# A fused two-layer block on one core: a position bias table made later, a triangle of ones loaded and copied earlier

## The chip, the core and the metric

The kernel runs on one core of a Trainium2 chip. Its engines have a queue each, which they work through in order: TensorE (PE, matmuls and transposes; its weight loads are PEld), VectorE (DVE), ScalarE (ACT), GpSimd (POOL) and SyncE (SP, which here only issues DMAs). The metric is the device time of one execution in microseconds (us), the median of several runs.

## The reference, cut to what matters

Two transformer blocks run one after the other on 512 tokens of width 1024, in float32. The change lies in the first 60 us of the first block, its input projection and the start of its attention:

```
xn   = rmsnorm(x, attn_norm_g)                       # 512 x 1024
proj = xn @ w_in                                     # 1024 -> 2312 columns
qa, ka, va, qb, kb, vb, f_logit = split(proj)
# mixer A: 8 heads, 2 key heads, window 128, a position bias per head, sinks
scores = qa . ka / 8  - 2^-(h+1) * dist              # dist = query - key, 0..127
out_a  = softmax with sink(scores) @ va
# mixer B: 8 heads, causal, forget gates
log_f  = log_sigmoid(f_logit + b_forget)             # 512 x 8
c      = cumsum(log_f, over tokens)
out_b  = softmax(qb . kb / 8 + c[t] - c[s], causal) @ vb
x      = x + concat(out_a, out_b) @ w_out
x      = x + relu(rmsnorm(x) @ w_up)^2 @ w_down
```

The second block (modulated norms, a pooling mixer, neighbourhood attention over the 512 tokens and a context, a second MLP) follows and isn't touched.

## The kernel before

Every float32 matmul is done as three passes: each operand is split into a rounded high part and a low rest, and `mm3` (lines 155 to 158) multiplies high by high, high by low and low by high into one accumulator. `split` (149 to 152) makes the parts: ACT copies to the high part, DVE (or POOL) subtracts for the low one.

`attention_one` does norm, projection and both mixers. The tokens stand in four tiles of 128 (t = 0 to 3). The projection is done in six chunks c of 384 or 392 columns (two for mixer A, four for B). `project(c, finish)` holds the loop: the weights of a chunk come in four pieces kp (`load`, `part_of`, 256 rows each), a raw DMA into one of two buffers, then a multiply by the norm's gain (L187 and L188, or on POOL, L185, for two of the four pieces) into a ring of five pairs `w_kp h/l`. For chunk 0 tiles 0 and 1 are multiplied as their tokens arrive, then tiles 2 and 3 one after the other. Each accumulator lies in one of two PSUM banks, so the matmuls of tile 2 need the bank that the eviction of tile 0 frees. The eviction is `close(t)`: one ACT operation (L411) that writes `pjs` and scales by the token's norm `r1[t]`, made by ACT (L260, a sum of squares) and two POOL operations (L208, L209). Then `finish` computes head norms on POOL, transposes q and k on PE (`ta`, L494) and evicts them as parts on ACT and DVE (L468 to L478). Between tile 2 and tile 3 the weights of the next chunk are loaded.

After chunk 0 the program makes the bias table `tab` (named alibi, L746: eight ACT copies of a 128x256 distance matrix `alibi0`, each with its head's slope), which DVE's pass over the scores `sa` (L609) adds. Then `gates()` turns the eight forget columns `zf` into log-sigmoids (Exp and Ln on ACT, L545 and L546), spreads them to `lfx`, splits that to `lfh`, and sums over tokens by a matmul `cps` (L562) with a triangle of ones `trir`: 896 columns loaded raw (`traw`, L556) and cast by DVE (L558). `lfx`, `traw` and `chl` come from one ring of three buffers (`prob("l", ..)`), `lfh` and `trir` from another (`prob("h", ..)`), in the order in which the program draws them; the input tiles `xin` and two raw weight pieces used the same rings before.

From there on attention of mixer A runs interleaved with the projection of the next chunk (generators, `interleave`), then mixer B with the rest.

The order in each engine's queue isn't that of the program. A planner runs the whole program at build time on a simulated clock and gives each engine, at each moment, the oldest of the operations that it holds for ready. Waits between engines are added afterwards. `tc.issue_after(ins)` is a rule for the planner: operations traced in its block on the engine of `ins` are queued behind `ins`; it adds no wait.

Of the kernel before, what the change touches and what calls it, by code (L numbers as in the profile page):

```python
# [8 lines left out]
F32 = mybir.dt.float32  # L9
F32R = mybir.dt.float32r  # L10
AF = mybir.ActivationFunctionType
# [5 lines left out]
P = 128  # L17
# [16 lines left out]
C_TRI = 384  # L34
# [99 lines left out]
class Build:  # L134
# [172 lines left out]
    def attention_one(self, ph):  # L307
        tc, nc, a = self.tc, self.nc, self.a
        tp = ph.enter_context(tc.tile_pool(name="t1", bufs=2, reuse_waits="tile"))
        cst = a["consts"]  # L310
        ac = nc.scalar.activation
# [3 lines left out]
        def const(name, shape, dt=F32):  # L315
            return tp.tile(shape, dt, name=name, tag=name, bufs=1)

        def prob(which, name, shape, dt=F32R):
            return tp.tile(shape, dt, tag="pt" + which, name=name, bufs=3)
# [17 lines left out]
        def load(c):  # L337
            tiles = []
            for kp in range(4):
                rv, (n, w, gain) = part_of(c, kp)  # L340
                tiles.append(self.parts(f"w{c}_{kp}", rv, n, w, gain, nc.gpsimd if c > C1 and kp in KPG else None))
                yield 0.0
            loaded[c] = tiles
# [18 lines left out]
        r1 = const("r1", [P, NT])  # L362
# [16 lines left out]
        alibi0 = const("alibi0", [P, 256])  # L379
# [9 lines left out]
        def project(c, finish):  # L389

            n = sum(w for _, w in segs[c])
            if c and c not in loaded:
                yield from load(c)
            tiles = loaded.pop(c) if c else []
            accs = {}

            def part(t, kp):
                if kp == 0:
                    accs[t] = self.ps("x", f"pj{c}_{t}")
                cols = slice(t * P, (t + 1) * P)  # L400
                wh, wl = tiles[kp]
                for i in range(2):
                    k = 2 * kp + i
                    xq = xnT[k // 4]
                    self.mm3(accs[t][:, 0:n], xq[:, k % 4, 0, cols], xq[:, k % 4, 1, cols], wh[:, i, :], wl[:, i, :],
                             k == 0, k == KC - 1)
                    yield 0.48

            def close(t):
                s = tp.tile([P, 392], F32, tag="pj", name=f"pjs{c}_{t}", bufs=2)  # L410
                ac(out=s[:, 0:n], in_=accs[t][:, 0:n], func=AF.Copy, scale=r1[:, t:t + 1])  # L411
                finish(t, s)

            def square(t):
                self.inv_rms(xin[t], r1, t, f"r1_{t}", self.part("wl", f"xs{t}", F32))

            turns = range(NT)
            if c == 0:
                turns = (2, 3)
                for kp in range(4):  # L420
                    if kp < 2:
                        self.split_T(xin[kp], xnT, kp, f"n1_{kp}")
                    rv, (a_, w, gain) = first[kp]
                    tiles.append(self.parts(f"w0_{kp}", rv, a_, w, gain))
                    if kp == 0:
                        yield from part(0, 0)
                    else:
                        if kp == 1:
                            yield from part(0, 1)
                            yield from part(1, 0)  # L430
                            yield from part(1, 1)
                        else:
                            square(kp - 2)
                            yield from part(0, kp)
                            yield from part(1, kp)
                for t in (2, 3):
                    self.split_T(xin[t], xnT, t, f"n1_{t}")
                for t in range(2):
                    close(t)
                    square(t + 2)  # L440
            for t in turns:
                for kp in range(4):
                    yield from part(t, kp)
                close(t)
                if t == NT - 2 and c + 1 < len(segs):
                    yield from load(c + 1)

        def head_norm(s, nh, name):

            w = 64 * nh  # L450
            sq = tp.tile([P, 384], F32, tag="sq", name=name + "sq", bufs=1)
            nc.gpsimd.tensor_tensor(out=sq[:, 0:w], in0=s[:, 0:w], in1=s[:, 0:w], op=ALU.mult)
            ss = self.small("ss", name + "ss")
            nc.vector.tensor_reduce(out=ss[:, 0:nh], in_=sq[:, 0:w].rearrange("p (h d) -> p h d", h=nh), axis=AX.X, op=ALU.add)
            r = self.rstd(ss[:, 0:nh], nh, 64, name + "r")
            qn = tp.tile([P, 384], F32, tag="qn", name=name + "qn", bufs=2)
            nc.gpsimd.tensor_tensor(out=qn[:, 0:w].rearrange("p (h d) -> p h d", d=64),
                                    in0=s[:, 0:w].rearrange("p (h d) -> p h d", d=64),
                                    in1=r[:, 0:nh].unsqueeze(2).to_broadcast([P, nh, 64]), op=ALU.mult)
            return qn  # L460
# [43 lines left out]
        def project_a(i):  # L504
            pa = Pairs(f"ta{i}")

            def finish(t, s):
                if i == 0:
                    nc.vector.tensor_tensor(out=zf[:, t, :], in0=s[:, 384:392], in1=bfor, op=ALU.add)
                qn = head_norm(s, 5, f"a{i}{t}")  # L510
                self.split(va[i][0][:, t, 0:64], va[i][1][:, t, 0:64], s[:, 320:384])
                pa.put(t, [qn[:, 0:P], qn[:, P:2 * P], qn[:, 2 * P:2 * P + 64]])
                if t % 2 == 1:
                    cols = slice((t - 1) * P, (t + 1) * P)
                    for h in range(4):
                        put_q(qa[4 * i + h], pa.get(h // 2), gn["q_norm_a"], h % 2, cols)
                    put_k(*ka[i], pa.get(2), gn["k_norm_a"], 0, cols, True)
            yield from project(i, finish)
# [22 lines left out]
        def gates():  # L541

            az = const("az", [P, NT, 8])
            stt(out=az, in0=zf, scalar=-1.0, in1=zf, op0=ALU.mult, op1=ALU.max)
            ac(out=az, in_=az, func=AF.Exp, scale=-1.0)  # L545
            ac(out=az, in_=az, func=AF.Ln, bias=1.0)  # L546
            stt(out=zf, in0=zf, scalar=0.0, in1=az, op0=ALU.min, op1=ALU.subtract)
            lfx = prob("l", "lfx", [P, NT, P], F32)
            lfh = prob("h", "lfh", [P, 2, NT, P])
            nc.gpsimd.memset(lfx, 0.0)  # L550
            for t in range(NT):
                nc.vector.tensor_copy(out=lfx[:, t, 0:32].rearrange("p (h r) -> p h r", r=4),
                                      in_=zf[:, t, :].unsqueeze(2).to_broadcast([P, 8, 4]))
            self.split(lfh[:, 0], lfh[:, 1], lfx)
            traw = prob("l", "traw", [P, 896], F32)
            nc.sync.dma_start(out=traw, in_=cst[:, C_TRI:C_TRI + 896])  # L556
            trir = prob("h", "trir", [P, 896])
            nc.vector.tensor_copy(out=trir, in_=traw)  # L558
            cps = self.ps("s", "cps")
            for t in range(NT):  # L560
                for part in range(2):
                    mm(out=cps, lhsT=lfh[:, part, t, :], rhs=trir[:, 384 - 128 * t:896 - 128 * t],  # L562
                       start=(t == 0 and part == 0), stop=(t == NT - 1 and part == 1))
            chl = prob("l", "chl", [P, 2, SEQ])
            self.split(chl[:, 0], chl[:, 1], cps)
            for dst, o in ((bq, 0), (bk, 3)):
                tmp = tp.tile([P, SEQ], F32, tag="p", name=f"btmp{o}", bufs=3)
                nc.vector.tensor_scalar(out=tmp, in0=chl[:, 0].bitcast(F32), scalar1=coef[:, o:o + 1],
                                        scalar2=coef[:, o + 2:o + 3], op0=ALU.mult, op1=ALU.add)
                stt(out=dst, in0=chl[:, 1].bitcast(F32), scalar=coef[:, o + 1:o + 2], in1=tmp, op0=ALU.mult, op1=ALU.add)  # L570
# [168 lines left out]
                    values(u, h)  # L739
                    yield CB * 0.8  # L740

        for _ in project_a(0):
            pass
        tab = self.gp.tile([P, 8, 256], F32, tag="g", name="alibi")
        for h in range(8):
            ac(out=tab[:, h, :], in_=alibi0, func=AF.Copy, scale=-(2.0 ** -(h + 1)))  # L746
        mixT.append(self.quad("mixT0"))
        b = {}
        gates()
        interleave(attn_a((0, 1)), project_a(1), RA[0])  # L750
        interleave(attn_a((2, 3)), project_b(0, b), RA[1])
# [799 lines left out]
```

## Time and profile before

| | |
|---|---|
| three runs | 1253.91, 1253.65, 1258.92 us, median 1253.91 |
| profiled execution | 1258.2 us, its span 1256.4 us, mean granted clock of PE 0.987 |
| PE busy | 1211.0 us, 96% of the span |
| DVE, ACT, POOL busy | 843.2 us (67%), 594.2 us (47%), 256.4 us (20%) |
| PE in the 40 slices of the span | 7899999998999999999999999999899999999997 |
| DMA | 155.42 MB, mean 124 GB/s |

A slice is 31.4 us and a digit its busy share in tenths. Busy shares are averages over stages with different limits: PE is the fullest engine in nearly all of them. In a timeline a row is one operation or several like it: start, length, engine, line, operation, tile written and tiles read, shapes, count, and in brackets the idle time of the engine ahead of it with what ended that.

### The profile page before, as it was taken

What the parts mean: (1) busy time and instruction counts of PE and PEld (TensorE: products, weight loads), DVE (VectorE), ACT (ScalarE), POOL (GpSimd) and SP (SyncE); (2) the same over time, 40 slices, a digit from 0 to 9 for tenths busy, and PEclk for the clock granted to TensorE, in tenths of its full rate; (3) what the DMA queues carried; (4) which work ended last, traced back from release to release, by engine and by line L of the source; (5) the groups of instructions that cost most, each with busy time, mean ns of one, the idle gap of its engine ahead of it and who ended that gap; (6) DMA issues with size and microseconds to landing.
All of it is one profiled execution on the core that took longest, in us unless ns stands there. A gap on an engine that the chain in (4) does not pass through costs nothing. (4 is left out here: it accounts for less than half of the span.)

```text
span 1256.4 us, 16975 instructions
## 1 busy us (share of the span) xinstructions
PE 1211.0 (96%) x6304; PEld 1013.8 (81%) x6304; DVE 843.2 (67%) x1461; ACT 594.2 (47%) x1103; POOL 256.4 (20%) x324
## 2 busy tenths in 40 slices
PE   7899999998999999999999999999899999999997
PEld 6898888788888878888889878777798888888775
DVE  3798776497988864346355557574867568578675
ACT  5576655434323313225245546463566454453442
POOL 2787552243010000000013224030600000000000
PEclk8998999999999999999999999999999999999998
DMA  6221222355668744234145311315355535436331
GB/s 165 64 59 46 66 63 68 101 167 149 206 217 258 235 138 141 67 101 135 67 151 158 85 51 53 102 38 201 119 189 161 166 86 177 142 98 187 101 101 67
DMA packets 154154, 155.42 MB, mean 124 GB/s; under 512 B 14489, under 2 KB 115624, under 8 KB 154072
## 3 DMA queue, kind: packets, MB, share of 16 engines
q1 hardware_dynamic: 149096, 143.08, 37.4%
q0 software_dynamic: 4400, 10.22, 2.6%
q8 instruction: 49, 0.80, 0.3%
q10 hardware_dynamic: 576, 1.05, 0.2%
q14 instruction: 33, 0.27, 0.1%
HBM read 147.96 MB, written 6.36 MB: 123 GB/s over the span
## 5 line engine op out<-in xcount | busy, mean ns | idle before, releaser
L902 DVE SCALAR_TENSOR_TENSOR macc<-mod,silu_c,macc 128x1024 f32<-128x1024 f32 x56 | 76.7, 1379 | 14.1 <-DMA mod<-in_w_mod_dram 14.1
L1453 POOL TENSOR_TENSOR ss<-ss,nhalf 128x1 f32<-128x1 f32 x4 | 3.0, 740 | 332.8 <-DVE ss L1452 332.8
L1305 DVE TENSOR_TENSOR m2d<-m2d,m2d 128x1024 f32<-128x1024 f32 x28 | 34.1, 1222 | 21.9 <-DMA m2d<-in_w_mlp_out_dram 21.8
L979 DVE SCALAR_TENSOR_TENSOR xa<-m1d,r,xa 128x512 f32<-128x512 f32 x32 | 23.8, 746 | 35.3 <-PE m1d L158 35.3
L151 ACT ACTIVATE m1hid<-m1sq 128x512 fp32r<-128x512 f32 x32 | 20.0, 630 | 37.4 <-DVE m1sq L848 37.4
L922 POOL DMA_DIRECT2D modrows<-mrow x8 | 3.9, 492 | 144.4 <-DVE mrow L920 90.2
L152 DVE TENSOR_TENSOR npl<-t,nph 128x512 fp32r<-128x512 f32 x32 | 21.7, 680 | 16.4 <-ACT nph L151 16.3
L152 DVE TENSOR_TENSOR m1hid<-m1sq,m1hid 128x512 fp32r<-128x512 f32 x32 | 21.9, 686 | 9.1 <-ACT m1hid L151 9.1
L185 POOL TENSOR_SCALAR w<-w,g_attn 128x384 f32<-128x384 f32 x20 | 25.6, 1290 | 8.9 <-DMA w<-in_w_in_dram 6.3
L687 DVE TENSOR_REDUCE mb<-sb 128x1 f32<-128x128 f32 (+3 forms) x32 | 15.6, 486 | 16.7 <-PE sb L684 16.6
L198 POOL TENSOR_SCALAR p<-p,d 128x512 f32<-128x512 f32 x8 | 14.0, 1752 | 55.8 <-DVE d L1120 26.5
L1119 ACT ACTIVATE p<-s,m 128x512 f32<-128x512 f32 x32 | 22.0, 689 | 5.8 <-DVE m L1117 5.8
L689 ACT ACTIVATE pb<-sb,mb 128x128 f32<-128x128 f32 (+3 forms) x32 | 16.8, 526 | 15.8 <-DVE mb L687 15.5
L847 ACT ACTIVATE m1re<-m1up 128x512 f32<-128x512 f32 x32 | 18.7, 583 | 11.0 <-PE m1up L158 11.0
L156 PE MATMUL pj<-w_0h,xnT 128*128 128x384 f32 (+1 forms) x48 | 18.5, 386 | 4.5 <-ACT pjs L411 3.3
L151 ACT ACTIVATE nph<-t 128x512 fp32r<-128x512 f32 x32 | 19.1, 596 | 7.4 <-PE t L1130 7.2
L1073 POOL TENSOR_TENSOR tb<-G,nam 128x256 f32<-128x256 f32 x24 | 17.8, 774 | 22.3 <-DVE m L1113 12.5
L848 DVE SCALAR_TENSOR_TENSOR m1sq<-m1up,m1re 128x512 f32<-128x512 f32 x32 | 21.8, 682 | 0.0
L1270 ACT ACTIVATE m2sq<-m2up 128x512 f32<-128x512 f32 x32 | 18.7, 584 | 6.5 <-PE m2up L158 6.5
L1331 DVE TENSOR_TENSOR y<-m2p,y 128x512 f32<-128x512 f32 x32 | 21.1, 682 | 0.2 <-PE m2p L158 0.2
L1272 ACT ACTIVATE m2sq<-m2sq 128x512 f32<-128x512 f32 x32 | 20.2, 633 | 0.9
L151 ACT ACTIVATE pbh<-tb 128x128 fp32r<-128x128 f32 (+3 forms) x32 | 13.7, 435 | 14.5 <-PE tb L707 14.4
(2045 smaller groups left out, 4624.3 us busy)
## 6 DMA issues: line engine op xcount, KB each, us to landing
m2d<-in_w_mlp_out_dram SPq DMA_DIRECT2D x53, 512.0 KB, 3.7
mod<-in_w_mod_dram SPq DMA_DIRECT2D x48, 512.0 KB, 4.4
m1u<-in_w_up_dram SPq DMA_DIRECT2D x32, 512.0 KB, 4.4
m1d<-in_w_down_dram SPq DMA_DIRECT2D x32, 512.0 KB, 3.6
m2u<-in_w_mlp_in_dram SPq DMA_DIRECT2D x32, 512.0 KB, 4.1
w<-in_w_in_dram SPq DMA_DIRECT2D x16, 512.0 KB, 4.0
w<-in_w_in_dram SPq DMA_DIRECT2D x48, 128.0 KB, 2.6
o1w<-in_w_out_dram SPq DMA_DIRECT2D x8, 512.0 KB, 3.7
```

Of the source, the lines that this page charges most:

```text
L151: self.nc.scalar.activation(out=hi, in_=src, func=AF.Copy)
L152: (eng or self.nc.vector).tensor_tensor(out=lo, in0=src, in1=hi.bitcast(F32), op=ALU.subtract)
L185: eng.tensor_scalar(out=rv[:, i], in0=rv[:, i], scalar1=g, scalar2=None, op0=ALU.mult)
L847: ac(out=r, in_=acc, func=AF.Relu)
L848: nc.vector.scalar_tensor_tensor(out=s, in0=acc, scalar=0.0, in1=r, op0=ALU.max, op1=ALU.mult)
L902: nc.vector.scalar_tensor_tensor(out=accs[s], in0=rw, scalar=sc[:, s, k:k + 1], in1=accs[s], op0=ALU.mult, op1=ALU.add)
L979: nc.vector.scalar_tensor_tensor(out=x[t][:, cols], in0=acc, scalar=r2[:, t:t + 1], in1=x[t][:, cols], op0=ALU.mult, op1=ALU.add)
L1119: ac(out=pr, in_=s, func=AF.Exp, bias=m[:, 2:3], accum_out=den[:, 0:1])
L1270: ac(out=s, in_=acc, func=AF.Relu)
L1272: ac(out=s, in_=s, func=AF.Square)
L1305: tt(out=o, in0=x, in1=z, op=ALU.subtract)
L1331: tt(out=Y[n][tau], in0=acc, in1=Y[n][tau], op=ALU.add)
```

## The change

It does three things. `close` keeps its eviction instruction in `self.closed`. The table's eight copies are traced in a block that queues them behind the last such eviction of chunk 0, that of tile 3. The draw, load and cast of the triangle move from the middle of `gates()` into the first projection: behind 32 steps of its generator, that is after the first half of tile 3's matmuls, behind the loads of chunk 1's weights.

```diff
             def close(t):
                 s = tp.tile([P, 392], F32, tag="pj", name=f"pjs{c}_{t}", bufs=2)
-                ac(out=s[:, 0:n], in_=accs[t][:, 0:n], func=AF.Copy, scale=r1[:, t:t + 1])
+                self.closed = ac(out=s[:, 0:n], in_=accs[t][:, 0:n], func=AF.Copy, scale=r1[:, t:t + 1])
                 finish(t, s)
...
             self.split(lfh[:, 0], lfh[:, 1], lfx)
-            traw = prob("l", "traw", [P, 896], F32)
-            nc.sync.dma_start(out=traw, in_=cst[:, C_TRI:C_TRI + 896])
-            trir = prob("h", "trir", [P, 896])
-            nc.vector.tensor_copy(out=trir, in_=traw)
             cps = self.ps("s", "cps")
...
-        for _ in project_a(0):
+        first_a = project_a(0)
+        for _ in range(32):
+            next(first_a)
+
+        traw = prob("l", "traw", [P, 896], F32)
+        nc.sync.dma_start(out=traw, in_=cst[:, C_TRI:C_TRI + 896])
+        trir = prob("h", "trir", [P, 896])
+        nc.vector.tensor_copy(out=trir, in_=traw)
+        for _ in first_a:
             pass
         tab = self.gp.tile([P, 8, 256], F32, tag="g", name="alibi")
-        for h in range(8):
-            ac(out=tab[:, h, :], in_=alibi0, func=AF.Copy, scale=-(2.0 ** -(h + 1)))
+        with tc.issue_after(self.closed.ins):
+            for h in range(8):
+                ac(out=tab[:, h, :], in_=alibi0, func=AF.Copy, scale=-(2.0 ** -(h + 1)))
```

## Rows read from the trace of the kernel before

**Rows 1.** Busy time by stretch: engines' busy us (operations), granted clock, DMA share, GB/s.

```profile
25.20:31.20 6.00, 6.00 (x18) 6.00 (x19) 3.28 (x8) 4.75 (x11) 5.66 (x8) 0.50 0.13 52
...
48.00:52.40 4.40, 4.10 (x12) 3.17 (x13) 3.64 (x11) 3.22 (x5) 3.43 (x3) 0.61 0.14 32
...
48.00:150.00 102.00, 97.91 (x630) 91.50 (x631) 89.22 (x281) 70.46 (x207) 75.92 (x85) 0.95 0.25 60
```

**Rows 2.** Timeline of PE, 21 to 48 us.

```profile
21.72 0.71 PE L220 MATMUL n_3t<-ident,xin 128*128 128x128 f32 x5
25.18 0.70 PE L156 MATMUL pj<-w_0h,xnT 128*128 128x392 f32 x1 [2.76 <-ACT pjs L411]
...
31.23 0.39 PE L156 MATMUL pj<-w_3h,xnT 128*128 128x392 f32 x1
...
32.36 0.35 PE L156 MATMUL pj<-w_0h,xnT 128*128 128x392 f32 x1
...
36.68 0.49 PE L494 MATMUL ta<-ident,a00qn 128*128 128x128 f32 x3
...
48.00 0.47 PE L562 MATMUL cps<-trir,lfh 128*128 128x512 f32 x1 [2.86 <-DVE trir L558]
```

**Rows 3.** Timeline of ACT, 22 to 47 us.

```profile
22.10 2.56 ACT L746 ACTIVATE alibi<-alibi 128x256 f32<-128x256 f32 x8 [2.78 <-DMA alibi<-in_consts_dram]
24.57 0.57 ACT L411 ACTIVATE pjs<-pj,r 128x392 f32<-128x392 f32 x1
25.04 1.11 ACT L187 ACTIVATE w_0h<-w,g_attn 128x384 fp32r<-128x384 f32 x2
...
38.79 1.12 ACT L187 ACTIVATE w_2h<-w,g_attn 128x384 fp32r<-128x384 f32 x2 [3.49 <-DMA w<-in_w_in_dram]
39.81 0.57 ACT L411 ACTIVATE pjs<-pj,r 128x392 f32<-128x392 f32 x1
41.51 0.47 ACT L468 ACTIVATE qa<-ta,misc 64x256 fp32r<-64x256 f32 x1 [1.13 <-PE ta L494]
...
46.72 0.63 ACT L151 ACTIVATE lfh<-lfx 128x512 fp32r<-128x512 f32 x1 [0.96 <-DVE lfx L552]
```

**Rows 4.** Timeline of SP's queue: DMA issues from 19 us on.

```profile
19.23 3.30 SPq L173 DMA_DIRECT2D w<-in_w_in_dram  x6
22.63 0.41 SPq L556 DMA_DIRECT2D traw<-in_consts_dram  x1
34.67 40.70 SPq L173 DMA_DIRECT2D w<-in_w_in_dram  x22
```

**Rows 5.** DMA issues, 0 to 80 us: count, KB each, median us to landing.

```profile
w<-in_w_in_dram SPq DMA_DIRECT2D x21, 128.0 KB, 2.6
...
traw<-in_consts_dram SPq DMA_DIRECT2D x1, 448.0 KB, 4.1
```

**Rows 6.** Timeline of POOL, 25 to 37 us.

```profile
25.93 2.48 POOL L185 TENSOR_SCALAR w<-w,g_attn 128x384 f32<-128x384 f32 x2
...
34.65 1.85 POOL L152 TENSOR_TENSOR w_1l<-w,w_1h 128x768 fp32r<-128x768 f32 x1 [0.58 <-ACT w_1h L151]
36.45 0.60 POOL L209 TENSOR_TENSOR r<-r_3ss,nhalf 128x1 f32<-128x1 f32 x1
```

**Rows 7.** Timeline of DVE, 33 to 48 us.

```profile
33.46 1.15 DVE L188 SCALAR_TENSOR_TENSOR w_0l<-w,g_attn,w_0h 128x384 fp32r<-128x384 f32 x2 [3.44 <-PE pj L157]
35.04 1.48 DVE L509 TENSOR_TENSOR zf<-pjs,misc 128x8 f32<-128x8 f32 x1 [0.43 <-ACT pjs L411]
...
47.23 0.63 DVE L558 CAST trir<-traw 128x896 fp32r<-128x896 f32 x1
```

**Rows 8.** Timeline of PE, 96 to 103 us.

```profile
96.42 0.69 PE L632 MATMUL ta<-ident,p 128*128 128x128 f32 x2 [2.49 <-DVE pal L152]
97.66 0.69 PE L156 MATMUL pj<-w_0h,xnT 128*128 128x384 f32 x1 [0.55 <-ACT pjs L411]
...
102.95 0.37 PE L157 MATMUL pj<-w_2l,xnT 128*128 128x384 f32 x1
```

## The prediction

> **What bounds the kernel now.** I read the profile in this order. First its page: TensorE (PE) is busy 96% of the span, and of its 40 slices the first two, one further on and the last are under 90%. Then the busy time by stretch [rows 1], cut along PE's timeline [rows 2]. PE has two holes early on: 2.76 us before 25.18, ended by ScalarE's (ACT) eviction `pjs`, and 2.86 us before 48.00, ended by VectorE's (DVE) cast `trir`. Behind them the granted clock is 0.50 (25.2 to 31.2 us) and 0.61 (48.0 to 52.4), that is wholly or mostly the 1.2 GHz level. Last the other engines around the holes [rows 3 to 7]. So at the start the path to the end runs through the order of queues and not through PE's rate; behind it PE has little idle time, and what the start gains or loses is handed on unless the attention stage swallows it.
>
> The first hole in detail. Program order puts the bias table (8 ACT operations) behind the whole first projection, yet in the trace they start at 22.10 and take 2.56 us, ahead of that projection's first eviction at 24.57 [rows 3]. So the order in a queue is the planner's: it takes what its own clock holds for ready, and it took the table's input for landed. On the chip ACT first stood idle 2.78 us for that DMA. PE ended its last transposes `n_3t` at 21.72 + 0.71 = 22.43 and went on at 25.18, in the bank that the eviction freed [rows 2].
>
> **The change part by part.**
>
> *The eviction comes forward.* Tied behind the last eviction, the table can't stand in front of the first. PE issued accumulator 0's last matmul before 21.72, and the eviction (0.57 us) had no wait of its own behind the table [rows 3]; without the table it can end by about 22.4, and PE has no reason to stop at 22.43: 25.18 - 22.43 = 2.75 us. Second, the clock: from 25.18 to 31.23 PE issued 18 projection matmuls in 6.05 us, while 24 of the same kind took 36.68 - 32.36 = 4.32 us, 0.18 each [rows 2]. At that rate the 18 cost 3.24 us, 2.81 less. PE would end the first projection 5.56 us earlier.
>
> *What is late next.* Not all of that passes. GpSimd (POOL) works almost without a break from 25.93 to 37.05 us: gain multiplies of the next weights, norms of the token tiles, the weights' low part `w_1l`, last the row scale `r_3` that the fourth eviction needs [rows 6]. That is 11.12 us with one idle piece of 0.58, so 10.54 of work. Its first multiply needs weights: their six issues run from 19.23 to 22.53, so the last starts at about 22.0, and such a transfer lands 2.6 us on [rows 4, 5], at 24.6. Then `r_3` is ready at 24.6 + 10.54 = 35.1. Before it was ready at 37.05, but the fourth eviction ran at 39.81 only, because ACT, in order, stood until 38.79 at weights whose DMA had been issued at 34.67 [rows 3, 4]. That DMA waits for a buffer that the fourth token tile's matmuls free (a wait of DVE's `w_0l` on PE, [rows 7]), so it moves with PE, and ACT is through with it at 39.81 - 5.56 = 34.3. The fourth eviction then follows `r_3` at about 35.2, 4.6 us earlier. This is the shift I carry on, not PE's 5.56.
>
> *The table itself* costs 2.56 us of ACT behind that eviction. There ACT has 1.13 us idle ahead of 41.51 [rows 3]; the other 1.43 pushes what follows: the evictions of q and k, then the gates' Exp and Ln and `lfh`, on which the second hole's matmul `cps` waits. Bounds: 0 if the planner spreads the eight over both idle pieces (1.13 and the 0.96 before 46.72) and what the shift opens; 2.56 if they stand in one block without cover. I take 1.43, the nearest to the rows as they stand. The table's first reader, DVE's pass over `sa`, comes behind `trir` in its queue, over 8 us later; it isn't late.
>
> *The triangle.* `cps` starts at 48.00, 0.14 us after `trir` ends (47.86) [rows 2, 7]. Its other operand `lfh` ends at 46.72 + 0.63 = 47.35 [rows 3]. With the cast done early, `cps` can follow at 47.49: 0.51 us earlier, no more, as `lfh` comes right behind. The cast stands late today because its tile comes from the ring of `lfh` and is drawn after it; the new place draws it first. Its DMA keeps its place at 22.63, behind chunk 1's weights and before those that wait until 34.67, and lands 4.1 us on, 26.7 [rows 4, 5]; if it were planned behind the others it would land by about 40, still before `cps`. The cast (0.63 us) fits into DVE's idle 3.44 us before 33.46 [rows 7]: nothing. Its worst place is at DVE's head, in front of the fourth tile's splits: DVE is held until 26.7 + 0.63 = 27.3, where PE wants that tile from 22.43 + 24 x 0.18 = 26.8. That, with the split behind it, is about the 1.0 us by which PE leads POOL's chain (5.56 against 4.6); some 0.3 could pass. Bounds: 0.51 won, 0.3 lost; I take 0.51. The memset of `lfx` shares a ring with the raw triangle and may leave POOL's idle time for its chain, at most the 0.6 us of a short POOL operation there [rows 6]; I take 0.
>
> The cast gets a neighbour. At 35.04 an add of 8 columns took DVE 1.48 us beside POOL's `w_1l` (34.65 to 36.50), while the cast of 896 columns took 0.63 where POOL had nothing to do [rows 6, 7]: the two engines slow each other. The Trainium skill, Advanced Engine Details and Errata, Mode Summary, says that a two-port VectorE operation and GpSimd share a port and block each other. By that rule the cast, set beside POOL's chain, would add up to its own length to that chain, and the sum below would be 3.1 instead of 3.7; the row shows the price on DVE's side only.
>
> *Sum.* 4.6 - 1.43 + 0.51 = 3.7 us earlier at `cps`. The hole in front of it doesn't shrink, since PE's own matmuls come earlier by about as much, and the half clock behind it stays. The profiled execution took 1258.2 us (span 1256.4, and 1.8 around it), 4.3 above the median of the runs, 1253.9; all rows are its own. By it the changed kernel takes 1254.5, and against the median 1253.9 - 3.7 = 1250.2 us.
>
> **Rivals.**
>
> *Full carry.* The planner orders POOL otherwise (norms during the wait for weights), the table fits into idle pieces, and all passes: 5.56 + 0.51 = 6.1, 1247.8. Since the whole order is planned anew, the stall before 96.42 may go too: 2.49 + 0.55 us idle, and 16 matmuls in 102.95 - 97.66 = 5.29 us instead of 2.88 [rows 8], 5.4 in all: 1242.4. For it: that stall is an accident of order. Against: no operation of the edit lies near it. 1247.6 or less has 0.23.
>
> *The gap stays, with another owner.* With the table gone, the planner may set the weight multiply `w_0h` (1.11 us, at 25.04 now) ahead of the evictions, as it did with the table. The third of the six issues starts at about 20.3 and lands at 22.9, the eviction runs at 24.0, and 0.6 us is won: 1253.3. For it: the planner has taken a DMA as landed too early before. Against: it sets an eviction in front of that multiply now [rows 3]. Chance 0.13.
>
> *Slower: a new stall in the attention stage.* Engines are in order and loaded there: of the 102 us from 48 on DVE is busy 89, POOL 76, PE 98 [rows 1]. A new order of `p` turns, splits and evictions can set PE in front of a late split a second time, as at 96.42. Price: the same 5.4 us, so 5.4 - 3.7 = 1.7 slower, 1255.6; two of them 1261. It decides from 3.7 us of new idle time and half clock between 48 and 150 us. For it: one such stall is there now. Against: only one in 102 us. Chance 0.19, of which 0.08 lies above 1260.2.
>
> **Numbers.** The forecast (1248 to 1252.5) has 0.45. What a measurement can't tell from no change is 0.5%, 1247.6 to 1260.2. Faster: 0.23 from the full carry and 0.01 of the forecast's edge, 0.24. Slower: 0.08 from new stalls, 0.01 from the rest, 0.09. Same: 0.67. The range takes in the second rival, part of the first and the single stall: 1245 to 1257.5.
>
> **What would show it.** Right: ACT's first `pjs` at 21 to 22 us, no PE hole at 22.4 and full clock from there to about 40; the table right behind the fourth `pjs`, at about 35; `trir` before 34; `cps` at about 44.3 and released by `lfh`; a PE hole of 3 to 4.5 us before it. Wrong: `pjs` later than 24; `cps` later than 47; POOL idle over 2 us between 24.6 and 35 (then the step with POOL is wrong and more is won); a PE idle piece over 2 us after 52 that isn't there now, or the one before 96.42 gone.

## The result, and the profile after

The changed kernel takes 1272.24 us (median, 1270.14 to 1273.5) against 1254.76 for the kernel before in the same series: ratio 1.0125, 95% interval 1.0106 to 1.0144. It is slower by 17.5 us, where 3.7 less was forecast and the range ended at 1257.5. The profiled execution took 1273.5 us (span 1271.7), against 1258.2 (1256.4) before.

The first stage did part of what it should. PE's timeline of the changed kernel, 20 to 50 us, answers to [rows 2]; a line gives start, duration, instruction, and in brackets the idle time in front of it and who ended it.

```profile
21.10 0.71 PE L220 MATMUL n_3t<-ident,xin 128*128 128x128 f32 x5
...
33.59 0.90 PE L494 MATMUL ta<-ident,a00qn 128*128 128x128 f32 x3 [2.99 <-POOL a00qn L457]
...
48.28 0.80 PE L558 MATMUL cps<-trir,lfh 128*128 128x512 f32 x1 [1.18 <-ACT lfh L151]
```

The hole of 2.76 us behind `n_3t` is gone. But PE meets a new one of 2.99 us at `ta`, which waits for POOL's `a00qn`; and `cps` starts at 48.28, not earlier than its 48.00 before. ACT's timeline (answers to [rows 3]):

```profile
20.45 0.59 ACT L411 ACTIVATE pjs<-pj,r 128x392 f32<-128x392 f32 x1 [1.74 <-PE pj L158]
23.16 1.13 ACT L187 ACTIVATE w_0h<-w,g_attn 128x384 fp32r<-128x384 f32 x2 [2.12 <-DMA w<-in_w_in_dram]
...
33.57 0.59 ACT L411 ACTIVATE pjs<-pj,r 128x392 f32<-128x392 f32 x1 [3.67 <-POOL a00qn L457]
...
38.78 0.59 ACT L411 ACTIVATE pjs<-pj,r 128x392 f32<-128x392 f32 x1 [1.97 <-POOL a01qn L457]
39.27 2.25 ACT L751 ACTIVATE alibi<-alibi 128x256 f32<-128x256 f32 x7
...
47.61 0.62 ACT L151 ACTIVATE lfh<-lfx 128x512 fp32r<-128x512 f32 x1
```

The first eviction comes 4.1 us earlier, the fourth only 1.0, and `lfh` 0.9 later. Not all of this stands clear of chance. Four experiments below (x_tail, x_den, b_xg, b_best) keep the first stage as it was; in their traces and in that of before the first eviction starts at 23.66 to 25.79 us, the fourth at 37.59 to 40.08, the first `sa` at 41.52 to 44.85, `lfh` at 43.90 to 46.99 and `cps` at 45.18 to 48.27. So only the first eviction is surely earlier, and nothing behind it is. POOL's timeline shows why (answers to [rows 6]):

```profile
26.19 2.83 POOL L185 TENSOR_SCALAR w<-w,g_attn 128x384 f32<-128x384 f32 x2 [4.35 <-DMA w<-in_w_in_dram]
...
34.65 1.82 POOL L152 TENSOR_TENSOR w_1l<-w,w_1h 128x768 fp32r<-128x768 f32 x1
36.43 0.93 POOL L209 TENSOR_TENSOR r<-r_3ss,nhalf 128x1 f32<-128x1 f32 x1
37.34 0.73 POOL L452 TENSOR_TENSOR a02sq<-pjs 128x320 f32<-128x320 f32 x1
38.03 0.72 POOL L457 TENSOR_TENSOR a01qn<-pjs,a01r 128x320 f32<-128x320 f32 x1
```

POOL stands idle for 4.35 us until the weights have landed, at 26.2, and then works through the same chain as before; `r_3` starts 0.02 us from its old time.

That explains a gain that fails to come, not a loss of 15 us. I cut the traces at the first score matmul (`sa`), the last, the last score matmul of mixer B (`sb`), and the first matmul of the accumulator `x`; the times are starts in the trace, each column the difference of two.

| profiled execution, us | first `sa` | mixer A: to last `sa` | mixer B: to last `sb` | dense: to first `x` | first `x` |
|---|---|---|---|---|---|
| before | 44.6 | 75.9 | 112.2 | 437.9 | 670.6 |
| after | 43.1 | 87.5 | 107.9 | 447.7 | 686.2 |
| difference | -1.5 | +11.6 | -4.3 | +9.8 | +15.6 |

From the first `x` to the last `m2d` both take the same, 576.3 and 576.0 us. So the loss stands in the mixers and in the dense stages, places that no line of the edit touches. The mixers must be read together: the new order puts 36 more of PE's matmuls in front of the last `sa` (477 against 441), and mixer B has 30 fewer. Together A and B lose 7.3 us. PE's larger idle pieces of the changed kernel there, from its timeline:

```profile
67.47 0.39 PE L601 MATMUL sa<-kah,qa 128*128 128x256 f32 x1 [1.39 <-ACT p L610]
...
79.48 0.38 PE L601 MATMUL sa<-kah,qa 128*128 128x256 f32 x1 [2.28 <-ACT p L610]
...
82.14 1.11 PE L628 MATMUL ta<-ident,p 128*128 128x128 f32 x4 [1.92 <-DVE pal L152]
...
104.07 0.48 PE L601 MATMUL sa<-kah,qa 128*128 128x256 f32 x2 [1.99 <-DVE qa L469]
...
293.29 1.09 PE L220 MATMUL n_1t<-ident,xg 128*128 128x128 f32 x4 [4.62 <-DVE xg L949]
...
459.76 0.50 PE L156 MATMUL m1d<-m1d100h,m1hid 128*128 128x512 f32 x1 [4.66 <-DVE xa L984]
```

Behind `cps`, mixer A had one such hole, of 2.49 us [rows 8]; it has four now, 7.58 us together. The dense stages had 3.93 us at `n_2t` and 1.19 at `m1d`; now 4.62 at `n_1t` and 4.66 at `m1d`. Busy time by stretch, mixer A and mixer B, before and then after (columns: PE, PE's weight loads, DVE, ACT, POOL, the granted clock, DMA share, GB/s):

```profile
44.59:120.48 75.89, 68.95 (x441) 65.85 (x441) 68.26 (x223) 53.22 (x155) 58.20 (x66) 0.93 0.22 53
120.48:232.69 112.21, 112.21 (x689) 94.19 (x688) 79.59 (x205) 67.26 (x178) 46.75 (x55) 1.00 0.20 56
...
43.10:130.60 87.50, 76.66 (x477) 73.66 (x478) 79.47 (x238) 57.75 (x167) 59.89 (x67) 0.90 0.20 46
130.60:238.50 107.90, 107.65 (x659) 89.62 (x657) 75.31 (x194) 64.12 (x171) 43.98 (x53) 1.00 0.20 58
```

In A PE is idle 10.8 us at a granted clock of 0.90, where it was idle 6.9 us at 0.93. The sequence of instructions differs in all queues: of PE's 6304, those from about number 174 to 2010 stand in another order, and of DVE's 1461 records in the trace 513 places hold another operation.

### The profile page after: what moved, and what is told of

It reads as the page before. It is cut to its first block, busy times and chain, and to the rows that moved or that the text cites. A ratio compares the mean times of both kernels' runs of the same rounds, so it can differ in the third digit from the quotient of the medians.

```text
span 1271.7 us, 16986 instructions
## 1 busy us (share of the span) xinstructions
PE 1215.1 (96%) x6304; PEld 1016.7 (80%) x6304; DVE 850.2 (67%) x1461; ACT 592.2 (47%) x1103; POOL 254.7 (20%) x324
## 5 line engine op out<-in xcount | busy, mean ns | idle before, releaser
L683 DVE TENSOR_REDUCE mb<-sb 128x1 f32<-128x128 f32 (+3 forms) x32 | 15.6, 488 | 13.3 <-PE sb L680 12.8
L152 DVE TENSOR_TENSOR pbl<-tb,pbh 128x128 fp32r<-128x128 f32 (+3 forms) x32 | 15.3, 482 | 9.2 <-ACT pbh L151 8.9
L411 ACT ACTIVATE pjs<-pj,r 128x384 f32<-128x384 f32 (+1 forms) x24 | 13.9, 580 | 16.1 <-PE pj L158 8.6
```

The source lines that it names most:

```text
L152: (eng or self.nc.vector).tensor_tensor(out=lo, in0=src, in1=hi.bitcast(F32), op=ALU.subtract)
```

## The experiments

Theory R: the edit itself is worth about nothing; the planner, given another program, orders some 1800 of PE's instructions behind it anew, and this order is worse. Theory D: the edit itself delays something. Most kernels below keep a given order: a function at the end draws an edge from each instruction to the next of a written list, without a wait.

```
         Build(tc, a, out).run()
+        pin(tc, nc)      # instruction k of ORDER stands behind instruction k-1
```

The traces show that the order holds: in x_tab DVE and POOL run the sequence of the kernel before without an exception, ACT but for the moved table, and PE but for two neighbours. Ratios are to the kernel before, with 95% intervals.

**The edit with the order held.** One part, or both, in the order of before:

```
x_tab:   ORDER of before, alibi[0..7] moved behind the fourth pjs
x_both:  the same, and traw's cast moved in front of DVE's w1_0l
x_head:  ORDER of after up to the first sa, then ORDER of before
x_tail:  ORDER of before up to the first sa, then ORDER of after (no edit)
```

x_tab: 

> Every queue keeps the order of the kernel before, drawn instruction by instruction; only the eight table copies stand elsewhere, in one block behind the fourth eviction. Theory R (the loss of 17 us comes from the planner's new order behind the first scores, and the edit itself moves the first 50 us by about a microsecond): the first PE hole closes, the fourth eviction comes about 1 us earlier because POOL's chain starts when weights land at 26 us and not sooner, the table takes that back: 1253 to 1257 us. Theory D (the edit itself costs the time: the table in front of the gates, PE running ahead into a hole before POOL's norms at half clock): 1262 us or more.

x_both: 

> As the one before, and the triangle's cast stands early too, in DVE's queue in front of the low part of the next weights' first piece; the memset of lfx stands behind the triangle's DMA. All other queue orders are those of the kernel before. Theory R: 1252 to 1256 us, some 0.5 us under the table's move alone. Theory D: 1262 us or more.

x_head: 

> The order of the changed kernel up to the first score matmul, and behind it, for every queue, the order of the kernel before. Theory R: the loss is gone, 1252 to 1257 us. Theory D: the loss stays, 1265 us or more, since the changed first 43 us are all there.

x_tail: 

> The opposite join: the order of the kernel before up to the first score matmul (table early, triangle's cast behind lfh), and behind it the order of the changed kernel. Theory R: slow without any of the edit in it, 1266 to 1273 us. Theory D: 1253 to 1258 us.

Measured: x_tab 1255.43 us, 0.9997 (0.9983 to 1.0010). x_both 1257.48, 1.0019 (1.0005 to 1.0034). x_head 1258.46, 1.0023 (1.0010 to 1.0036). x_tail 1269.62, 1.0120 (1.0100 to 1.0141). The kernel without a line of the edit, but with the new order behind the first scores, has the whole loss; the edit with the old order has none (x_tab) or about 0.2% (x_both and x_head, clear of zero). As the cause of the 17 us, D falls. x_tab and x_tail lie in their windows of theory R; x_both and x_head lie 1.5 us above theirs, far under those of D. The missing gain of 3.7 us is a question of its own, below.

**Where the new order costs.**

```
x_att:  ORDER of after up to the first output projection, then of before
x_den:  ORDER of before up to the first output projection, then of after
```

x_att: 

> Every queue holds the order of the changed kernel up to the first output projection of the attention stage, and the order of the kernel before behind it; both parts of the edit are in it. If the loss is made where the attention's scores run (the holes ahead of the score matmuls that wait for exp on ScalarE and for qa), it keeps most of it: 1266 to 1272 us. If the later stages' new order makes it (the wait of the first dense matmuls for the input that VectorE splits, xa), it keeps only what attention A and B lose by their end, 5 to 6 us: 1260 to 1264. If the tail's order matters nowhere alone: 1255.

x_den: 

> The mirror of the run before: the order of the kernel before up to the first output projection, the changed kernel's order behind it. If attention's order makes the loss: 1254 to 1258 us. If the dense stages' order makes a part of it by the wait of m1d for xa (4.7 us in the changed kernel, 1.2 before) and the following: 1260 to 1265. The two gains over before should add up to the 16 us of the whole.

x_att 1265.2 us, 1.0074 (1.0047 to 1.0101); x_den 1265.43, 1.0071 (1.0048 to 1.0094). Half and half; the two, 9.5 and 9.7 us, add up to 19.2 where the whole is 17.5, which their intervals allow. Both expectations missed narrowly: x_att lies between its two windows, 0.8 us under the upper one, and x_den 0.4 us above its own. Their profiled executions agree with the table above: mixer A lasts 84.7 us in x_att and 75.6 in x_den, the dense stages 436.8 and 443.9.

**Is it this edit, or any?**

```
n_swap (the edit is not in it; planned freely)
-        nc.sync.dma_start(out=alibi0, in_=cst[:, C_ALIBI:C_ALIBI + 256])
...
         nc.sync.dma_start(out=ctmp, in_=cst[:, C_CAUS:C_CAUS + P])
+        nc.sync.dma_start(out=alibi0, in_=cst[:, C_ALIBI:C_ALIBI + 256])
f_tri:  only the triangle's part of the edit, planned freely
f_tab:  only the table's part, planned freely
```

n_swap: 

> The kernel before with no part of the edit: only two constants' loads, the slopes of the position bias and the causal triangle, are issued in swapped order, and the whole program is planned anew from there. The theory that a new plan alone costs or gives microseconds: the time differs from before by at least 3 us in either direction, with the first order difference some way behind the swap, PE holes at other places behind 45 us, and the first 40 us as before. The theory that the edit itself costs: within 1.5 us of 1255.

f_tri: 

> Only the triangle's part of the edit (loaded early, copied by VectorE during the first projection), the rest planned freely. The triangle's copy itself is worth nothing by the sum (0.5 us at most). If the plan decides: a third time, at least 3 us from 1255 or from 1272, the holes behind 45 us at places of its own. If the table's move is what costs: 1255 within 1.5 us.

f_tab: 

> Only the table's part of the edit, planned freely; its queues nearly equal the changed kernel's. If the new plan makes the loss, it is here whole: 1269 to 1273 us, with the four holes between 44 and 105 us and that of m1d near 460 us. If the triangle's part is needed for it: 1255 to 1260.

n_swap 1267.84 us, 1.0092 (1.0066 to 1.0117): two loads that change places cost nearly as much as the edit. f_tri 1260.14, 1.0036 (1.0022 to 1.0050). f_tab 1272.03, 1.0113 (1.0099 to 1.0128): the kernel with the table's part alone, planned anew, has the whole loss. f_tri and f_tab came out as the theory of the plan had them. Four plans of nearly the same work (before, f_tri, n_swap, f_tab) thus lie between 1255 and 1272 us. One statement of the n_swap expectation failed: its first 40 us are not as before, `cps` runs ahead of the scores and the first `sa` starts at 49.6. By the last `sb` its trace is only 1.4 us behind that of before (234.1 against 232.7); the dense stages then take 443.9 us instead of 437.9. DVE's queue in n_swap, ahead of the same `m1d`:

```profile
443.27 1.27 DVE L902 SCALAR_TENSOR_TENSOR macc<-mod,silu_c,macc 128x1024 f32<-128x1024 f32 x1
447.34 1.28 DVE L902 SCALAR_TENSOR_TENSOR macc<-mod,silu_c,macc 128x1024 f32<-128x1024 f32 x1 [2.80 <-DMA mod<-in_w_mod_dram]
449.59 1.28 DVE L902 SCALAR_TENSOR_TENSOR macc<-mod,silu_c,macc 128x1024 f32<-128x1024 f32 x1 [0.96 <-DMA mod<-in_w_mod_dram]
450.79 2.06 DVE L979 SCALAR_TENSOR_TENSOR xa<-m1d,r,xa 128x512 f32<-128x512 f32 x3
```

The eviction `xa`, which frees PE's bank, stands behind two products that wait 2.80 and 0.96 us for a DMA. In the changed kernel the same lines read 2.74 and 0.79 us, with `xa` at 458.96 and `m1d` at 459.76.

**One place at a time.** Single DVE instructions moved, in the order of after (a_) or of before (b_):

```
a_xa:   after;  xa0 moved in front of the two waiting macc
a_fix:  a_xa;  va1l behind ma, ea (hole at 67.47); two sa passes behind the
        first ma, ea (79.48); two w_0l behind pal (82.14); two w_2l behind qa (104.07)
b_xg:   before; xg12 moved in front of two macc (hole of 3.93 us at n_2t)
b_best: b_xg;  xa0 in front of one macc; two w_2l behind pal (hole at 96.42)
```

a_xa: 

> The changed kernel's order with one VectorE instruction moved: the eviction xa of the first accumulator goes in front of the two macc products that wait for a DMA (2.74 and 0.79 us in the changed kernel). If that one place makes the stall of m1d: the PE hole of 4.66 us falls to 1.3 or less and the half clock behind it (some 1.2 us) goes, 4.5 to 5.3 us in all: 1267 us. If the stall has another cause (the accumulator's own matmuls, or a DMA that everything waits for): 1271 to 1273.

1267.74 us, 1.0081 (1.0068 to 1.0094), as expected; the interval lies wholly under the changed kernel's (1.0106 to 1.0144). DVE's and PE's timelines of a_xa:

```profile
452.32 0.75 DVE L983 SCALAR_TENSOR_TENSOR xa<-m1d,r,xa 128x512 f32<-128x512 f32 x1 [0.24 <-PE m1d L158]
454.84 1.28 DVE L906 SCALAR_TENSOR_TENSOR macc<-mod,silu_c,macc 128x1024 f32<-128x1024 f32 x1 [1.76 <-DMA mod<-in_w_mod_dram]
```

```profile
454.69 0.40 PE L158 MATMUL m1d<-m1d103h,m1hid 128*128 128x512 f32 x1
454.93 0.39 PE L156 MATMUL m1d<-m1d100h,m1hid 128*128 128x512 f32 x1
```

`m1d` follows without a hole, at full rate (0.23 us apart, where the first ten behind the hole took 3.99 us, 0.40 each). The dense stages' share falls from 447.7 to 441.2 us. This place is shown.

a_fix: 

> The run with xa moved (1267.7 us), and seven more VectorE instructions of the changed kernel's queue in the attention stage moved behind the ones that PE waits for: a split of v behind the row maximum and its exponent, two score passes behind the first row maximum, two weight splits behind pal, two behind qa. If the loss there is made by those places: the holes of 1.39, 2.28, 1.92 and 1.99 us shrink to 2.5 us in all, and with the half clock behind them 4 to 7 us go: 1261 to 1264 us. If something common to the stage makes them, the holes move on: 1266 to 1268.

1264.51 us, 1.0073 (1.0055 to 1.0092), between its two windows, 0.5 us above the lower one. The holes shrank from 7.6 to 5.2 us (2.58, 1.08, 0.94 and a new one of 0.62; 2.5 in all were expected) and mixer A from 87.5 to 83.4 us in the traces, but the ratio's interval covers that of a_xa: the gain in total time is not shown. The hole at 79 us withstood. There ACT's `p`, which ends PE's wait, itself waits for DVE's `ma`. DVE and POOL there, first in the changed kernel and then in a_fix:

```profile
77.27 1.32 DVE L608 TENSOR_SCALAR ma<-ma 128x2 f32<-128x2 f32 x1
```

```profile
76.76 1.80 POOL L152 TENSOR_TENSOR w_3l<-w,w_3h 128x768 fp32r<-128x768 f32 x1
```

```profile
70.71 0.16 DVE L608 TENSOR_SCALAR ma<-ma 128x2 f32<-128x2 f32 x1
...
76.65 1.76 DVE L608 TENSOR_SCALAR ma<-ma 128x2 f32<-128x2 f32 x1
```

```profile
76.59 1.79 POOL L152 TENSOR_TENSOR w_3l<-w,w_3h 128x768 fp32r<-128x768 f32 x1
```

`ma` starts 0.62 us earlier than in the changed kernel and ends 0.18 earlier, at 78.41; POOL's split ends at 78.38. In the changed kernel the two end at 78.59 and 78.56. By these rows the split holds it, not its place in DVE's queue; no run moved the split.

b_xg: 

> The kernel before, without the edit, with one VectorE instruction moved: the product xg of the third token tile's second half goes in front of two macc products (6.31 us together beside GpSimd's work). If an instruction's place behind longer work is what makes such holes: the hole of 3.93 us before n_2t and the half clock behind it (some 1.6 us) go: 1249 to 1251 us. If the following stages only take the gain back (the next xg becomes late): 1254 to 1256.

1258.67 us, 1.0009 (0.9994 to 1.0023): no gain. The hole of 3.93 us is gone, and PE has two others close by:

```profile
284.98 0.38 PE L156 MATMUL m1up<-hT,m1u3h 128*128 128x256 f32 x1 [1.19 <-ACT m1u3h L151]
287.48 0.58 PE L157 MATMUL m1up<-hT,m1u0h 128*128 128x256 f32 x1 [1.99 <-DVE hT L152]
```

PE then lacks other input (`m1u3h`, `hT`), as the second expectation had it in kind (its 1254 to 1256 us were some 3 too low).

b_best: 

> The run before, and two more places of VectorE: xa of the first m1d in front of one macc, and two weight splits w_2l behind the probabilities' low part pal on which PE waits 2.49 us in the attention stage. Each shortens its hole by 1 to 1.5 us, with the half clock behind it up to 2.5: 1245 to 1248 us, under both the kernel before and the changed one. If holes only move on: 1250 or more.

1254.9 us, 0.9992 (0.9974 to 1.0009): the second outcome, not told apart from before. No version here beats both kernels by a measurable amount.

**The gain that didn't come.**

```
x_pool: x_both; POOL: a00qn, r_3, a01r, a01qn ahead of w_1's gain multiply and w_1l;
        ACT: third and fourth pjs ahead of w_1h
```

x_pool: 

> The kernel before's order with both parts of the edit (1257.5 us), and one change of order at the first stage: GpSimd makes the norms a00qn, r_3 and a01qn ahead of the next weights' gain multiply and low part, and ScalarE takes the third and fourth eviction ahead of the next weights. If GpSimd's queue held the gain back, as the prediction's step says: the fourth eviction comes at 32 to 33 us and not at 38.0, the hole before ta closes, the wait for lfh too, and 3 to 4 us are won: 1253 to 1255 us. If the weights' low part becomes late instead (36 us and later): 1256 to 1259.

1258.36 us, 1.0024 (1.0009 to 1.0040): the second outcome. ACT and PE:

```profile
32.94 0.59 ACT L411 ACTIVATE pjs<-pj,r 128x392 f32<-128x392 f32 x1 [1.57 <-POOL a01qn L457]
35.40 0.84 ACT L151 ACTIVATE w_1h<-w 128x768 fp32r<-128x768 f32 x1 [1.87 <-POOL w L185]
```

```profile
36.29 0.69 PE L156 MATMUL pj<-w_1h,xnT 128*128 128x384 f32 x1 [2.83 <-ACT w_1h L151]
38.19 0.69 PE L157 MATMUL pj<-w_1l,xnT 128*128 128x384 f32 x1 [1.21 <-POOL w_1l L152]
...
47.70 0.50 PE L558 MATMUL cps<-trir,lfh 128*128 128x512 f32 x1 [1.21 <-ACT lfh L151]
```

The fourth eviction comes at 32.94, 5.1 us earlier than in x_both (38.01), and PE pays for it at once with 4.04 us of waiting for the weights that POOL makes later. `cps` comes at 47.70, against 46.11 in x_both, both within the 45.18 to 48.27 that the first stage without the edit has.

## Why the prediction was wrong

*"The eviction comes forward", 5.56 us at PE*: right against this one trace. The first `pjs` starts at 20.45, no hole follows, and the first projection's last matmul starts at 30.26 instead of 36.50. That is 6.24 us, of which 0.62 lie ahead of the change (`n_3t` at 21.10, not 21.72). But the 2.81 us of it that the clock gave are no steady price of the hole. Behind holes of 2.46 to 3.10 us in the same place and the same order, the 18 matmuls took 3.33 us in x_tail, 3.31 in b_best, 4.86 in x_den and 4.87 in b_xg, where they took 6.05 in before. The hole in b_best, the stretch behind it, and the changed kernel's stretch that answers to [rows 1]:

```profile
24.71 0.44 PE L156 MATMUL pj<-w_0h,xnT 128*128 128x392 f32 x1 [3.10 <-ACT pjs L411]
```

```profile
24.70:30.70 6.00, 5.99 (x33) 5.99 (x34) 3.81 (x9) 5.05 (x12) 5.63 (x8) 1.00 0.12 46
```

```profile
25.20:31.20 6.00, 5.40 (x30) 4.80 (x28) 3.27 (x7) 3.74 (x8) 4.68 (x6) 1.00 0.07 27
```

*"Such a transfer lands 2.6 us on, at 24.6"*: wrong; the first failed term. The row taken [rows 5] is of 128 KB loads, and the six issues there are two pieces of one 256 KB and two 64 KB loads each, which landed 3.9 and 3.3 us on in the trace before. After (the DMA issues from 0 to 80 us: count, KB each, median us to landing):

```profile
w<-in_w_in_dram SPq DMA_DIRECT2D x6, 256.0 KB, 4.7
w<-in_w_in_dram SPq DMA_DIRECT2D x12, 64.0 KB, 3.8
```

POOL waited for them until 26.19. By that start alone the step gives `r_3` at 26.2 + 10.5 = 36.7; it ended at 37.4.

*"The fourth eviction then follows `r_3`"*: wrong as well. `pjs` has two buffers, and the fourth tile's needs the one that `a01qn` reads; POOL does that two operations behind `r_3`, until 38.75, where the eviction starts at 38.78. That is 1.0 us earlier than in the trace of before, not 4.6. This bound stood in the trace of before, too, where ACT's wait for weights hid it, and in b_best, with the first stage of before, the fourth eviction waits for `a01qn` as well, and runs no later. POOL in before and ACT in b_best:

```profile
37.70 0.73 POOL L457 TENSOR_TENSOR a01qn<-pjs,a01r 128x320 f32<-128x320 f32 x1
```

```profile
38.08 0.59 ACT L411 ACTIVATE pjs<-pj,r 128x392 f32<-128x392 f32 x1 [1.75 <-POOL a01qn L457]
```

So the 4.6 us carried into the sum were nothing that these traces tell from chance. x_pool shows the layer below: put the norms first, and the weights are late. Whichever comes first, POOL's work between the weights' landing and `w_1l` sets the pace.

*The table*: 2.25 + 0.41 us behind the fourth eviction, where 2.56 were read. From that eviction to `qa` it is 2.64 us now (38.78 to 41.42) and was 1.70 (39.81 to 41.51): 0.94 where 1.43 were taken. *The triangle*: `trir` at 27.12, in front of `n_3t`'s second split, the place called the worst; `cps` was released by `lfh`, as forecast. `lfh` itself came late, because the planner set `w_3h` and `w_0h`, 1.9 us of ACT, ahead of it.

*The cast's neighbour*: `trir` took 0.79 us (0.63 before) and POOL's multiply beside it 2.83 instead of 2.48. The pair took 2.82 or 2.83 us in each of the six traces with the cast beside it, and 2.46 to 2.52 in the other ten. So POOL pays too, 0.35 us of the 0.6 that the rule of the Trainium skill, Advanced Engine Details and Errata, Mode Summary (two-port VectorE operations and GpSimd block each other), had given.

*The sum*: of the 3.7 us at `cps` none is shown. `cps` starts at 48.28 in the changed kernel and, where the order is held, at 47.25 in x_tab and 46.11 in x_both; with the first stage of before it starts at 45.18 to 48.27. Of the hole that was expected to stay in front of `cps`, 2.99 us have moved to `ta` and 1.18 us remain.

*The step that decided*: "Slower: a new stall in the attention stage", priced at 5.4 us each, one or two of them, with a chance of 0.19. Right in kind and far too small: mixer A got three holes more (A and B together lose 7.3 us), the dense stages a longer one at `m1d`. The working looked at 48 to 150 us only and said "against: only one in 102 us"; but the order is drawn anew for some 1800 of PE's instructions, up to 460 us and beyond, and half of the loss (x_den 1.0071) lies where no rival looked. The forecast itself assumed without saying so that the old order stays behind `cps`: it put the price of a new order at nothing, and that price was 1.0120 (x_tail, without the edit). For that case, too, it was 3 to 5 us low: against the medians of their own series x_tab is 0.6 us under the kernel before and x_both 1.5 above.

Open: the cause of the loss in mixer A, place by place. a_fix removed two of its holes in the trace and not a measurable time. Also open is how much of the dense stages' 9.8 us is chance. With the old order there they took 434.6 to 439.5 us in the profiled executions of six kernels (before, x_tab, x_both, x_head, x_att, x_pool), with the new one 443.9 to 447.7 in three (x_den, x_tail, the changed kernel): the two stay apart, by 4.4 us at least. The prediction's reading of the 40 slices missed one: two further on are under 90%, not one; nothing hangs on it.

## What to carry to other kernels

Where a planner orders the queues, an edit has two prices: its own, which the rows give, and that of a new order for all that follows, which they don't; here the second was about 1%, and two swapped loads showed it without any edit. Measure the second by itself: pin the old order and move only the edited instructions, or let a neutral edit be planned anew. And before a wait is counted as won, look for the next bound on the same instruction, its buffer's last reader above all, and take a landing time from the row with the transfer's own size. One trace is one execution: with the order of the first stage unchanged, `cps` moved by 3.1 us between five traces, as much as the gain that was forecast there.

## What the runs showed of the hardware

A VectorE operation on 128x2 elements (`ma`) takes 0.16 us in one place and 1.32 and 1.76 us in two others (changed kernel and a_fix), where it ends within 0.03 us of GpSimd's split `w_3l`. It does not run slower there in proportion; it ends when GpSimd's operation ends. This is no single case: in the first 260 us of the 16 traces 51 such `ma` took 0.5 us or more, and each ended within 0.05 us of the end of a GpSimd operation. The rule of the Trainium skill named above has the two block each other, and the trace agrees. Not every GpSimd operation does it, though: the `ma` of 0.16 us in a_fix ran at 70.71, while GpSimd worked on `a12r` (128x5, from 69.72 to 70.91). What these rows add is that a tiny operation can pay as much as a large one. In the two places named above `ma` was on the path to a PE hole (2.28 us at `sa` in the changed kernel, 2.58 in a_fix).

One and the same order of instructions is granted different clocks. Behind a hole of 2.46 to 3.10 us at one place, PE went on at a granted clock of 1.00 in two traces (x_tail, b_best) and of 0.50 in that of before, with x_den and b_xg between (3.31 to 6.05 us for the same 18 matmuls, as above); why is not shown. In the 19 runs of before next to x_att the quickest, 1252.74 us, had a mean granted clock of 0.995 and the slowest, 1261.22, 0.987.
